# A diffusion-transformer block: the starting addresses of matmul operands, shifted by unused columns in three pools

## The chip, the cores and the metric

The kernel runs on one core of one Trainium2 chip. The metric is the device time of one execution in microseconds (us). A core has TensorE (PE, with its weight loads shown apart as PEld), VectorE (DVE), ScalarE (ACT), GpSimd (POOL) and SyncE (SP, which here issues nearly all DMAs). SBUF is the core's working memory of 128 partitions; a tile takes the same bytes at the same address in every partition. An address below is the offset in bytes within a partition.

## The reference, cut to what matters

One layer, 2048 latent tokens of 1024 channels, preceded by 256 context tokens that only feed the state of the scan:

```
proj = (x * (1 + scale1) + shift1) @ w_in              # input projection
mix  = concat([conformer_conv(proj), ssd_both_directions(proj), pool_mixer(proj)])
x    = layer_norm(ALPHA * x + gate1 * (mix @ w_out))   # output projection
h    = x * (1 + scale2) + shift2
val, gate = split(h @ w_up)                            # up projection, 2 x 2816 columns
f    = (val * gelu(depthwise_conv_3x3(gate))) @ w_down # down projection
out  = layer_norm(ALPHA * x + gate2 * f)
```

Everything is in float32.

## The kernel before

Tokens go in four chunks of 512. A first sweep (`sweep1`, `chunk`, up to about 740 us) makes the input projection chunk by chunk, runs the convolutions on VectorE, the forward scan and the pooling, and parks results in DRAM. A second sweep runs backwards over the chunks: the backward scan (`bwd`), then the output projection and the first layer norm (`mix`). From about 1080 us the feed-forward part (`ffn_chunk`) follows, chunks 3, 2, 1, 0: for each of 22 blocks `f` of 128 columns the gate (`ug`) and the value (`uv`) of the up projection, with the depthwise convolution on VectorE (`fa`) between them; then for each half of the output columns the down projection (`d`) over the 22 blocks into four PSUM banks, then the second layer norm.

Each float32 product is made of three matmuls. `split` cuts an operand into a high part in the type that TensorE takes in one pass (`F32R`) and a remainder (ScalarE copies, GpSimd subtracts; for `gl` VectorE subtracts), and `mm3` multiplies high by high (L108), high by low (L109) and low by high (L110). Names say which: `wh`/`wl` are the halves of a weight tile, `hhi`/`hlo` of the activations of the input projection, `yah`/`yal` and `ybh`/`ybl` of the mixers' outputs, `h2h`/`h2l` of the activations of the up projection, `gh`/`gl` of the gated product. `proj` and the up projection hold the weights stationary (128 columns at a time) and move 512 columns of activations. `mix` and the down projection hold the activations stationary and move 512 columns of weights.

The instructions of every engine are ordered by the scheduler of the framework when the kernel is built. Tiles come from pools; a pool gives each tag its slots one behind the other, and pools stack from the low end or, with `side="right"`, from the high end. All weights go through `load_w` and the pool `wp`, whose slots start at 64 modulo 256. A slice of an operand starts a multiple of 256 bytes into its tile (512 k for a block of 128 columns, 2048 for half of a weight tile, 256 for the row of tokens ahead of a chunk), so an operand's place modulo 256 is that of its tile. In the built programs the operands of the four projections stand at:

| matmuls | stationary | moving | modulo 256 before | modulo 256 after |
|---|---|---|---|---|
| input projection `ps_x`, `ps_z`, `ps_a`, `ps_g`, `ps_p`, `ps_cx` | `wh`, `wl` | `hhi`, `hlo` (pool `p1`) | 64 and 0 | 64 and 64 |
| output projection `o` | `yah`, `yal`, `ybh`, `ybl` (pools `p2`, `pa`) | `wh`, `wl` | 160 and 64 | 64 and 64 |
| up projection `ug`, `uv` | `wh`, `wl` | `h2h`, `h2l` (pool `p3`) | 64 and 64 | 64 and 64 |
| down projection `d` | `gh`, `gl` (pool `p4`) | `wh`, `wl` | 224 and 64 | 64 and 64 |

The other tiles of these pools move along: in `p1` by 64 bytes up (`gl`, `pb`, `zt` and the mixers' weights), in `p2` and `pa` by 96 down (`xt`, `yfr`, `ngr` and others), in `p4` by 160 down (`g`, `r` and the rows of the layer norm). The matmuls of the small projection `dt_c` have 40 stationary columns whose slices are 160 bytes apart. The tiles of the activations are 2048 bytes apart in `p1`, `p2`, `pa` and `p4`; those of the up projection hold 576 columns and are 2304 bytes apart.

Of the kernel before, what the change touches and what calls it, by code (L numbers as in the profile page):

```python
# [7 lines left out]
F32 = mybir.dt.float32  # L8
# [5 lines left out]
P = 128  # L14
# [34 lines left out]
class Kern:  # L49
# [3 lines left out]
    def run(self):  # L53
        tc, t = self.tc, self.t
        with ExitStack() as es:
            self.cp = es.enter_context(tc.tile_pool(name="cp", bufs=1))
            self.wp = es.enter_context(tc.tile_pool(name="wp", bufs=2))
            self.lp = es.enter_context(tc.tile_pool(name="lp", bufs=2))
            self.mm = es.enter_context(tc.tile_pool(name="mm", bufs=4, space=PSUM))
            for n, b in (("si", 1), ("so", 2), ("lo", 1)):  # L60
                setattr(self, n, es.enter_context(tc.tile_pool(name=n, bufs=b, space=PSUM)))
            self.consts()
            e1, e2, e3 = ExitStack(), ExitStack(), ExitStack()
            self.sp = e1.enter_context(tc.tile_pool(name="sp", bufs=2))
            self.ssd_consts()
            e4, e5 = ExitStack(), ExitStack()
            self.pc = e5.enter_context(tc.tile_pool(name="pc", bufs=2, side="right"))
            self.mod_first()
            self.p1 = e4.enter_context(tc.tile_pool(name="p1", bufs=2))
            self.sweep1()  # L70
            e5.close()
            self.pa = e2.enter_context(tc.tile_pool(name="pa", bufs=2, side="right", reuse_waits="tile"))
            self.ngr = self.row(self.pa, t["norm_row"], "ngr")
            top = self.bwd(NCH - 1)
            e4.close()
            self.p2 = e2.enter_context(tc.tile_pool(name="p2", bufs=2, side="right", reuse_waits="tile"))
            last = self.sweep2(top)
            e1.close()
            self.p3 = e3.enter_context(tc.tile_pool(name="p3", bufs=2, reuse_waits="tile"))
            self.mix(*last)  # L80
            pre = self.ffn_pre()
            e2.close()
            self.p4 = e3.enter_context(tc.tile_pool(name="p4", bufs=2, side="right", reuse_waits="tile"))
            self.ffn(pre)
            e3.close()

    def bank(self, pool, name):
        return pool.tile([P, 512], F32, tag="b", name=name)

    def col(self, n, i):  # L90
        return self.cols[:, COFF[n] + i : COFF[n] + i + 1]
# [960 lines left out]
```

## Time and profile before

| | us |
|---|---|
| median of 3 runs (lowest to highest) | 2638.94 (2635.89 to 2642.15) |
| the profiled execution, its own time | 2638.48 |
| span in its trace, first to last instruction | 2636.8 |
| TensorE busy | 2430.4 (92% of the span) |
| VectorE busy | 1849.2 (70%) |
| GpSimd busy | 1330.7 (50%) |
| ScalarE busy | 1145.9 (43%) |
| mean granted clock of TensorE | 0.96 of full speed |

The times are of the whole execution; the trace is of one execution, and its span lacks what lies before the first and behind the last instruction. Busy time of TensorE runs from the start of a matmul to its end, and matmuls overlap: one of 512 columns lasts 0.39 us in the trace and the next starts before it ends. What a matmul costs in a stream is therefore read from the distance between two starts, not from its length. A granted clock of 1.00 is 2.4 GHz, one of 0.50 is 1.2 GHz.

### The profile page before, as it was taken

What the parts mean: (1) busy time and instruction counts of PE and PEld (TensorE: products, weight loads), DVE (VectorE), ACT (ScalarE), POOL (GpSimd) and SP (SyncE); (2) the same over time, 40 slices, a digit from 0 to 9 for tenths busy, and PEclk for the clock granted to TensorE, in tenths of its full rate; (3) what the DMA queues carried; (4) which work ended last, traced back from release to release, by engine and by line L of the source; (5) the groups of instructions that cost most, each with busy time, mean ns of one, the idle gap of its engine ahead of it and who ended that gap; (6) DMA issues with size and microseconds to landing.
All of it is one profiled execution on the core that took longest, in us unless ns stands there. A gap on an engine that the chain in (4) does not pass through costs nothing.

```text
span 2636.8 us, 31624 instructions
## 1 busy us (share of the span) xinstructions
PE 2430.4 (92%) x11338; PEld 1983.4 (75%) x11338; DVE 1849.2 (70%) x2681; ACT 1145.9 (43%) x1761; POOL 1330.7 (50%) x928
## 2 busy tenths in 40 slices
PE   6897999899767988899999999999999999899996
PEld 3776767677656766789998878888878888788885
DVE  5898978689966686576555496665696654876645
ACT  2656565756454333433334333344333343233332
POOL 2555464554524555554446455464454464555444
PEclk7998999999978999899999999999999999999998
DMA  7645343333336565562224343343333343433332
GB/s 281 209 151 170 101 133 124 120 119 111 116 124 211 180 212 189 175 212 92 88 88 131 91 149 97 98 125 100 120 127 97 97 120 94 146 96 104 96 98 70
DMA packets 125838, 347.01 MB, mean 132 GB/s; under 512 B 19680, under 2 KB 24176, under 8 KB 125680
## 3 DMA queue, kind: packets, MB, share of 16 engines
q1 hardware_dynamic: 121072, 336.60, 40.0%
q10 hardware_dynamic: 4608, 8.39, 1.1%
q8 instruction: 89, 1.46, 0.2%
q14 instruction: 69, 0.57, 0.1%
HBM read 298.63 MB, written 46.31 MB: 131 GB/s over the span
## 4 chain that ended last, share of the span: by engine, by line
PE 58%; DVE 23%; ACT 5%; DMA 5%; issue 4%; POOL 3%; SPq 0%; ACTq 0%; POOLq 0%; DVEq 0%
PE d L109 6%; PE d L108 6%; PE d L110 6%; PE uv L108 5%; PE uv L110 5%; PE uv L109 5%; PE ug L108 5%; PE ug L110 5%; PE ug L109 5%; DVE ca_f L256 2%; DVE ca_b L256 2%; DVE c31p L582 2%; DVE fa L876 1%; ACT E_f L345 1%; DVE xt L773 1%
## 5 line engine op out<-in xcount | busy, mean ns | idle before, releaser
L876 DVE SCALAR_TENSOR_TENSOR fa<-gbuf,cols,fa 128x512 f32<-128x512 f32 x704 | 523.5, 753 | 223.9 <-ACT fa L872 201.4
L906 DVE TENSOR_TENSOR gl<-g,gh 128x512 fp32r<-128x512 f32 x176 | 196.2, 1124 | 231.1 <-ACT gh L905 213.9
L96 POOL TENSOR_TENSOR wl_d<-wr_d,wh_d 128x1024 fp32r<-128x1024 f32 x88 | 218.1, 2479 | 227.0 <-ACT wh_d L95 227.0
L96 POOL TENSOR_TENSOR wl_uv<-wr_uv,wh_uv 128x1024 fp32r<-128x1024 f32 x88 | 221.8, 2521 | 203.7 <-ACT wh_uv L95 203.7
L108 PE MATMUL ug<-h2h,wh_ug 128*128 128x512 f32 (+3 forms) x880 | 308.5, 351 | 14.5 <-DVE g L884 10.6
L96 POOL TENSOR_TENSOR wl_ug<-wr_ug,wh_ug 128x1024 fp32r<-128x1024 f32 x88 | 215.1, 2444 | 189.1 <-ACT wh_ug L95 189.0
L109 PE MATMUL ug<-h2l,wh_ug 128*128 128x512 f32 (+3 forms) x880 | 307.4, 349 | 0.0
L110 PE MATMUL ug<-h2h,wl_ug 128*128 128x512 f32 (+3 forms) x880 | 307.1, 349 | 0.0
L108 PE MATMUL uv<-h2h,wh_uv 128*128 128x512 f32 x704 | 275.7, 392 | 10.0 <-DVE g L884 10.0
L109 PE MATMUL d<-wl_d,gh 128*128 128x512 f32 x704 | 280.6, 399 | 0.0
L108 PE MATMUL d<-wh_d,gh 128*128 128x512 f32 x704 | 277.3, 394 | 0.0
L109 PE MATMUL uv<-h2l,wh_uv 128*128 128x512 f32 x704 | 275.4, 391 | 0.0
L110 PE MATMUL uv<-h2h,wl_uv 128*128 128x512 f32 x704 | 275.2, 391 | 0.0
L110 PE MATMUL d<-wh_d,gl 128*128 128x512 f32 x704 | 266.0, 392 | 0.0
L905 ACT ACTIVATE gh<-g 128x512 fp32r<-128x512 f32 x176 | 110.9, 630 | 261.5 <-PE d L109 240.1
L108 PEld LDWEIGHTS ug<-h2h,wh_ug 128*128 128x128 f32 x880 | 167.4, 190 | 34.7 <-DVE g L884 11.8
L95 ACT ACTIVATE wh_ug<-wr_ug 128x1024 fp32r<-128x1024 f32 x88 | 93.2, 1059 | 220.1 <-PE uv L109 193.3
L109 PEld LDWEIGHTS ug<-h2l,wh_ug 128*128 128x128 f32 x880 | 167.3, 190 | 17.8
L110 PEld LDWEIGHTS ug<-h2h,wl_ug 128*128 128x128 f32 x880 | 167.2, 190 | 16.8
L582 DVE SCALAR_TENSOR_TENSOR c31p<-gl,cols,c31p 128x512 f32<-128x512 f32 x232 | 161.8, 745 | 12.2 <-ACT c31p L579 12.0
L108 PEld LDWEIGHTS uv<-h2h,wh_uv 128*128 128x128 f32 x704 | 132.8, 189 | 37.8 <-DVE g L884 11.0
L108 PEld LDWEIGHTS d<-wh_d,gh 128*128 128x128 f32 x704 | 132.1, 188 | 34.3
(388 smaller groups left out, 5536.7 us busy)
## 6 DMA issues: line engine op xcount, KB each, us to landing
wr_ug<-in_w_up SPq DMA_DIRECT2D x88, 512.0 KB, 3.6
wr_uv<-in_w_up SPq DMA_DIRECT2D x88, 512.0 KB, 3.6
wr_d<-in_w_dn SPq DMA_DIRECT2D x88, 512.0 KB, 3.5
wm<-in_w_mod SPq DMA_DIRECT2D x64, 256.0 KB, 3.6
wr_x<-in_w_x SPq DMA_DIRECT2D x32, 512.0 KB, 3.7
wr_o<-in_w_o SPq DMA_DIRECT2D x32, 512.0 KB, 4.2
wm<-in_w_mod SPq DMA_DIRECT2D x16, 512.0 KB, 8.3
x_c<-in_xT SPq DMA_DIRECT2D x32, 256.0 KB, 3.4
```

The lines of the kernel that those rows point to most:

```text
L95: nc.scalar.activation(hi, src, AF.Copy)
L96: nc.gpsimd.tensor_tensor(lo, src, hi.bitcast(F32), AL.subtract)
L108: nc.tensor.matmul(out, a[0], b[0], start=first, stop=False)
L109: nc.tensor.matmul(out, a[0], b[1], start=False, stop=False)
L110: nc.tensor.matmul(out, a[1], b[0], start=False, stop=last)
L256: nc.vector.scalar_tensor_tensor(acc[:, :n], raw[:, off : off + n], wk, acc[:, :n], AL.mult, AL.add)
L345: nc.scalar.activation(E[:, h, :], E[:, h, :], AF.Relu, bias=cum[:, d, s, h : h + 1], scale=-1.0)
L582: nc.vector.scalar_tensor_tensor(to[:, :m], gl[:, j, o + k : o + k + m], w[k], acc[:, :m], AL.mult, AL.add)
L773: nc.vector.scalar_tensor_tensor(xs[i][:, hsl], xs[i][:, hsl], ALPHA, m, AL.mult, AL.add)
L876: nc.vector.scalar_tensor_tensor(acc, G[:, dr : dr + 8, dc : dc + GW], wc[i], acc, AL.mult, AL.add)
L905: nc.scalar.activation(gh, gt[k], AF.Copy)
L906: nc.vector.tensor_tensor(gl, gt[k], gh.bitcast(F32), AL.subtract)
```

## The change

Three tiles that nothing writes or reads are added, each with a name of its own and one slot: 64 bytes in `p1`, 96 bytes in `pa`, 160 bytes in `p4`. The `p1` tile is the first of its pool, so that all others start 64 bytes later. `pa`, `p2` and `p4` grow from the high end, and the tile added there moves the tiles of the pool, and of the pool that stacks on it, 96 or 160 bytes down.

```diff
             self.p1 = e4.enter_context(tc.tile_pool(name="p1", bufs=2))
+            self.shift(self.p1, 64)
             self.sweep1()
...
             top = self.bwd(NCH - 1)
+            self.shift(self.pa, 96)
             e4.close()
...
             self.ffn(pre)
+            self.shift(self.p4, 160)
             e3.close()
...
+    def shift(self, pool, n):
+        pool.tile([P, n // 4], F32, name="shift", bufs=1)
```

In the built programs every engine has the same instructions in the same order with the same waits before and after (10767 on TensorE, 2683 on VectorE, 1779 on ScalarE, 933 on GpSimd, 849 on SyncE); the source lines behind the added ones shift by 2 to 6, and the addresses differ as the table above says. No row of the order stands here, since none differs in more than its line.

## Rows read from the trace of the kernel before

**Rows 1.** The page: its span, and busy us (share of the span) of TensorE.
```profile
span 2636.8 us, 31624 instructions
...
PE 2430.4 (92%) x11338; PEld 1983.4 (75%) x11338; DVE 1849.2 (70%) x2681; ACT 1145.9 (43%) x1761; POOL 1330.7 (50%) x928
```

**Rows 2.** The chain of waits over the whole span: shares by engine and line.
```profile
by line: PE d L109 6.2%; PE d L108 6.1%; PE d L110 6.1%; PE uv L108 5.2%; PE uv L110 5.1%; PE uv L109 5.1%; PE ug L108 5.0%; PE ug L110 5.0%; PE ug L109 5.0%; issue 4.1%; DVE ca_f L256 2.5%; DVE ca_b L256 2.4%; DVE c31p L582 2.0%; DVE fa L8
```

**Rows 3.** TensorE's timeline, up projection: start us, us, operation; 132 matmuls apart.
```profile
1660.05 0.39 PE L110 MATMUL ug<-h2h,wl_ug 128*128 128x512 f32 x1
...
1689.97 0.39 PE L110 MATMUL uv<-h2h,wl_uv 128*128 128x512 f32 x1
```

**Rows 4.** TensorE's timeline, down projection: 120 matmuls apart.
```profile
1771.53 0.39 PE L108 MATMUL d<-wh_d,gh 128*128 128x512 f32 x1
...
1799.53 0.39 PE L108 MATMUL d<-wh_d,gh 128*128 128x512 f32 x1
```

**Rows 5.** TensorE's timeline, input projection: 24 matmuls apart.
```profile
451.95 0.39 PE L110 MATMUL ps_x<-hhi_c,wl_x 128*128 128x512 f32 x1
...
457.55 0.39 PE L110 MATMUL ps_x<-hhi_c,wl_x 128*128 128x512 f32 x1
```

**Rows 6.** TensorE's timeline, output projection: 18 matmuls apart.
```profile
884.43 0.40 PE L108 MATMUL o<-wh_o,yah 128*128 128x512 f32 x1
...
888.65 0.40 PE L108 MATMUL o<-wh_o,yah 128*128 128x512 f32 x1
```

**Rows 7.** The same at half clock, 3 matmuls apart, and the window's PEclk.
```profile
861.50 0.63 PE L110 MATMUL o<-wh_o,yal 128*128 128x512 f32 x1
...
862.78 0.63 PE L110 MATMUL o<-wh_o,yal 128*128 128x512 f32 x1
...
core 0: us, PE busy (x) PEld busy (x) DVE busy (x) ACT busy (x) POOL busy (x), PEclk, DMA share, GB/s
860.50:863.00 2.50, 2.50 (x7) 1.92 (x7) 2.50 (x4) 1.01 (x1) 1.81 (x2) 0.50 0.95 336
```

**Rows 8.** Groups by form: `d` on L109 (busy us, mean ns); L108, L110 count alike.
```profile
L109 PE MATMUL d<-wl_d,gh 128*128 128x512 f32 x704 | 280.6, 399 | 0.0
```

**Rows 9.** TensorE's timeline, 448 columns in the last chunk: 21 matmuls apart.
```profile
2399.89 0.36 PE L110 MATMUL ug<-h2h,wl_ug 128*128 128x448 f32 x1
...
2404.15 0.36 PE L110 MATMUL ug<-h2h,wl_ug 128*128 128x448 f32 x1
```

**Rows 10.** Windows, a stretch of `d` alone: length, then columns as in rows 7.
```profile
1770.00:1860.00 90.00, 90.00 (x388) 72.39 (x387) 43.79 (x45) 37.35 (x51) 46.49 (x21) 1.00 0.38 112
```

**Rows 11.** Waits from 1760 to 1900: waiter, releaser, total us, times, longest.
```profile
ACT gh L905 <- PE d L109: 56.8, 33, 4.7
```

**Rows 12.** The chain in order of time behind the last `d` of chunk 3.
```profile
1508.45 0.24 PE d L110
1508.72 0.69 DVE fm L920
```

**Rows 13.** The chain's shares in windows 112:740, 228:300, 380:430 and 740:1076, in this order.
```profile
by line: DVE ca_f L256 10.3%; DVE ca_b L256 10.0%; DVE c31p L582 8.4%; issue 8.4%; ACT E_f L345 4.0%; DVE c31t L582 2.7%; PE ps_z L110 2.3%; PE ps_z L109 2.2%; PE ps_z L108 2.2%; POOL hlo_c L96 2.2%; DMA E_f<-scr_arow 1.7%; ACT L346 1.6%; D
by line: DMA x_c<-in_xT 9.1%; POOL hlo_c L96 8.3%; PE ps_x L108 6.2%; PE ps_x L110 6.1%; issue 5.9%; PE ps_x L109 5.8%; PE ps_a L110 5.2%; PE ps_a L108 5.2%; PE ps_a L109 5.2%; PE yd_f L408 4.7%; ACT E_f L345 3.2%; PE pl L665 2.8%; PE ps_g 
by line: DMA E_f<-scr_arow 10.9%; issue 9.4%; POOL hlo_c L96 9.2%; PE ps_a L108 8.2%; PE ps_a L109 7.1%; PE ps_a L110 6.9%; POOL wl_g L96 4.7%; ACT E_f L345 4.2%; PE ps_g L108 3.7%; PE ps_g L110 3.7%; PE ps_g L109 3.7%; ACT x_c L234 3.5%; P
by line: issue 8.0%; DVE xt L773 5.3%; DMA yac<-scr_yac 4.4%; DVE st_l L790 3.8%; PE o L108 3.8%; PE o L109 3.4%; DVE E_b L359 3.2%; DMA yfr<-scr_yf 3.0%; PE o L110 2.9%; PE st_b L390 2.7%; DVE mix L772 2.7%; DMA E_b<-scr_arow 2.6%; DMA xt<
```

**Rows 14.** TensorE's timeline, 256 columns: context 15 apart, up projection 21 apart.
```profile
79.15 0.28 PE L110 MATMUL ps_cx<-hhi_ctx,wl_cx 128*128 128x256 f32 x1
...
80.85 0.28 PE L110 MATMUL ps_cx<-hhi_ctx,wl_cx 128*128 128x256 f32 x1
...
1201.40 0.28 PE L110 MATMUL ug<-h2h,wl_ug 128*128 128x256 f32 x1
...
1203.92 0.28 PE L110 MATMUL ug<-h2h,wl_ug 128*128 128x256 f32 x1
```

## The prediction

> **What bounds the kernel now.** I read the page's busy times first: TensorE is busy 2430 of 2637 us [rows 1], so the question is whether the change makes its matmuls shorter, and where TensorE sets the end. The chain of waits answers the second: the down projection alone, `d`, holds 6.2 + 6.1 + 6.1 = 18.4% of the span, 485 us, and the up projection (`ug`, `uv`) some 30% more [rows 2]. Then I read TensorE's timeline for the one thing that the change could touch, the distance from the start of one matmul to the start of the next in an unbroken stream.
>
> All the streams in question are the same instruction: 128 rows, 128 stationary columns, 512 moving columns. The up projection starts one every (1689.97 - 1660.05) / 132 = 226.7 ns [rows 3]. The down projection starts one every (1799.53 - 1771.53) / 120 = 233.3 ns [rows 4], the input projection every (457.55 - 451.95) / 24 = 233.3 ns [rows 5], the output projection every (888.65 - 884.43) / 18 = 234.4 ns [rows 6]. Where the granted clock is 0.50, after a wait, the output projection takes (862.78 - 861.50) / 3 = 426.7 ns [rows 7], which is 512 columns at 1.2 GHz with nothing over. At 2.4 GHz the columns alone would be 213.3 ns, so at the full clock each matmul has 13.3 ns over in the up projection and 20.0 to 21.1 ns in the three others. The overhead does not scale with the clock, so it is not the array's own work; it looks like operands that arrive too slowly.
>
> Now the placement in the section on the kernel: in the up projection both operands start at 64 modulo 256; in the three others one starts at 64 and the other at 0, 160 or 224. The input projection and the up projection are the same code (`mm3` with the weights stationary, the same weight slots, the same PSUM pool), and they differ only in where the activations lie. So the trace of before already holds the experiment that the change makes on the other three.
>
> **The change part by part.** No instruction is added, removed or reordered, and every wait is as before; the only thing that changes is the address of the tiles of `p1`, `p2`, `pa` and `p4`. So nothing new can queue, and the sum is a length per matmul times the matmuls on the path.
>
> - Down projection. 704 matmuls on each of three lines, 2112 in all [rows 8]. If they go from 233.3 to 226.7 ns, all of them give 2112 x 6.67 ns = 14.1 us. On the chain they hold 485 us, so 485 x 20/700 = 13.9 us reaches the end. I take 13.9. The lower bound comes from a place where equal addresses gained less: the 448-column matmuls of the up projection in the last chunk run at (2404.15 - 2399.89) / 21 = 202.9 ns, 16.2 over their 186.7 [rows 9]; with 16.2 over, `d` would gain 3.8 ns each, 8.0 us.
>  Does the gain stay? In a stretch of 90 us that is nothing but `d`, TensorE is busy all 90 while VectorE is busy 43.8, ScalarE 37.4 and GpSimd 46.5 [rows 10], and it is ScalarE that waits for `d` to free the buffers of `gh`, 56.8 us in 140 [rows 11]. The feeders have room for a stream that is 3% faster. Behind the last `d` of a chunk the chain goes on through `fm` on VectorE [rows 12], which starts that much earlier.
> - Input projection. 18 tiles x 4 chunks x 8 x 3 = 1728 matmuls of 512 columns, at most 1728 x 6.67 = 11.5 us. But in the sweep the chain is VectorE's convolutions above all [rows 13]. What these rows show of it on the chain is `ps_z` 6.7% of 628 us, 42 us; `ps_x` and `ps_a` 33.7% of 72 us, 24 us; `ps_a` and `ps_g` 33.3% of 50 us, 17 us. Of these 83 us, 20/700 is 2.4 us. I take that; the bounds are 0 (the other engines take over) and 11.5.
> - Output projection. 768 matmuls, at most 768 x 7.7 = 5.9 us; on the chain 10.1% of 336 us, 34 us [rows 13], of which 7.7/234.4 is 1.1 us. I take 1.1; the bounds are 0 and 5.9.
> - Context tiles. Here the rule runs the other way. At 256 columns the input projection with 0 against 64 starts one every (80.85 - 79.15) / 15 = 113.3 ns, and the up projection with equal addresses one every (1203.92 - 1201.40) / 21 = 120.0 ns [rows 14]. If the 144 context matmuls go to 120, that is 1.0 us, partly on the path; I take half, 0.5 us lost.
> - The rest. The transposes `yt` (64) and `ht` (128) now have both operands at 160 and get 64 against 160; even at 6.7 ns each that is 1.3 us, taken at nothing, because their stage waits for others [rows 13]. The 96 matmuls of `dt_c` have slices at eight different places before and after: nothing. VectorE, ScalarE and GpSimd read and write the same tiles at a new place; in `d` they have the room of [rows 10], and I have no row that shows them depend on it: nothing.
>
> Sum: 13.9 + 2.4 + 1.1 - 0.5 = 16.9 us. The profiled execution took 2638.5 us (the median of the three runs is 2638.9, so it stands for them). 2638.5 - 16.9 = 2621.6, 0.64% less. A measurement of this kernel tells about 0.2%, 5.3 us, from no change.
>
> A rule speaks against all of this. The overhead over 213.3 ns in [rows 3 to 6], and its absence at the half clock in [rows 7], say that two streams of operands do get in each other's way. The Trainium skill (page "SBUF — State Buffer", section "Who interferes with whom") gives TensorE two independent read ports, one for the moving operand and one for the weight load, and says that TensorE never waits on anyone; "TensorE: Matmul & The Clock Gate", section "Back-to-back issue gap", gives columns over clock plus 2.5 ns, an estimate of 215.8 ns for 512 columns wherever they lie. By these pages the sum would be nothing, and the time 2638.5. The trace disagrees on the gap (226.7 and 233.3), so the ports are less free than that here.
>
> **The rivals.**
> 1. No change: place modulo 256 isn't the cause. The activations of the up projection are also 2304 bytes apart (576 columns), those of the three others 2048; a cause in the higher bits of the address would fit [rows 3 to 6] as well, and the change leaves those bits nearly alone. Against it: within the up projection the higher bits differ from one k to the next, and the interval does not. Time 2638.5, with the rest of the list within 2 us of it.
> 2. Slower: equal places collide. [rows 14] show it at 256 columns: +6.7 ns where the addresses are equal. If at 512 columns with the roles swapped (in `d` the activations are stationary and the weights stream) the overhead goes up a step instead of down, 2112 x 6.67 = 14.1 us are lost in `d` and 1.1 in the output projection, with 2.4 gained in the input projection as in the sum: 2638.5 + 12.8 + 0.5 = 2651.8. It decides if `d` starts one matmul less often than every 233.3 ns. Against it: 30 us of [rows 3] at 512 columns without an exception.
> 3. All of it comes through: the projections' gain isn't lost beside VectorE, because the chain there changes hands often. 14.1 + 11.5 + 5.9 - 0.5 = 31.0 us, 2607.5. Against it: only 17 us of the chain's 50 us by [rows 13] is TensorE's projections where `ps_a` and `ps_g` are at their densest.
> 4. Part of it: the streams fall into the pattern of [rows 9]. The three matmul terms shrink to 3.8/6.67: 17.4 x 0.57 - 0.5 = 9.4 us, 2629.1.
>
> **How the numbers follow.** The forecast (interval falls to about 226.7 in `d`, 13 to 24 us gained) 0.70; rival 4 0.10; rival 3 0.04; rival 1 0.11; rival 2 0.05. Forecast, 3 and 4 are faster by over 0.2%: 0.84; rival 1 is within 0.2%: 0.11; rival 2 slower: 0.05. The forecast's own range is 2614 to 2627. The range that should hold 8 in 10 goes down to rival 3, 2608, and up past rival 4 to 2636; outside lie rivals 1 and 2.
>
> **What would show each step.** In the timeline of the changed kernel, `d` should start a matmul every 226.7 ns (680 for a triple instead of 700), and the same for `ps_x`, `ps_z` and `o` where they run unbroken at the full clock; at the half clock they should stay at 426.7. Context matmuls at 120 ns. Mean length of the three `d` groups lower by some 6 ns each, and the up projection's as before. A 90 us stretch of `d` should still show TensorE busy throughout; if idle time appears in it, the feeders were the cover I misjudged. From the start of the first `ug` to the end the stretch should be 14 us shorter, and from the start to there about 3 us. I would be wrong if `d` stays at 233.3 (rival 1), rises (rival 2), or if the interval falls and the end doesn't move.

## The result and the profile after

| us | before | changed |
|---|---|---|
| median of 7 runs each | 2642.15 | 2629.33 |
| lowest to highest | 2635.89 to 2646.07 | 2621.35 to 2632.03 |
| the profiled execution, its own time | 2638.48 | 2625.29 |
| span in its trace | 2636.8 | 2623.6 |

The ratio of the two kernels is 0.9948 with a 95% interval of 0.9932 to 0.9964. Of 2642 us that is 13.7 us less, 9.5 to 18.0. The forecast was 16.9 us less, 2621.6 us. The time lies inside the range of 2608 to 2636 and 2 us above the 2614 to 2627 that the forecast's own mechanism was given. The kernel before stood at 2642.15 here, 3.7 us above the 2638.5 from which the sum was made.

The page of the changed kernel answers to [rows 1]; the second line is the head of the chain of waits over the whole span, which answers to [rows 2]. The source lines of `mm3` are now L114 to L116 (before L108 to L110).

```profile
PE 2419.6 (92%) x11338; PEld 1996.2 (76%) x11338; DVE 1840.7 (70%) x2681; ACT 1145.5 (44%) x1761; POOL 1336.3 (51%) x928
...
by line: PE d L114 5.8%; PE d L116 5.8%; PE d L115 5.8%; PE ug L114 5.3%; PE ug L115 5.3%; PE ug L116 5.3%; PE uv L114 5.2%; PE uv L115 5.2%; PE uv L116 5.1%; issue 4.1%; DVE ca_f L262 2.3%; DVE ca_b L262 2.3%; DVE fa L882 1.4%; DVE c31p L5
```

The same instructions were executed. The down projection holds 17.4% of the chain instead of 18.4%, and its place as the longest item did not pass to another engine.

TensorE's timeline of the changed kernel (start us, us, operation) shows what became of the streams of [rows 4], [rows 5], [rows 6] and the context part of [rows 14]. The pairs of rows are 131, 36, 15 and 15 matmuls apart.

```profile
1770.03 0.39 PE L114 MATMUL d<-wh_d,gh 128*128 128x512 f32 x1
...
1799.72 0.39 PE L114 MATMUL d<-wh_d,gh 128*128 128x512 f32 x1
```
```profile
449.50 0.39 PE L116 MATMUL ps_x<-hhi_c,wl_x 128*128 128x512 f32 x1
...
457.66 0.39 PE L116 MATMUL ps_x<-hhi_c,wl_x 128*128 128x512 f32 x1
```
```profile
887.12 0.40 PE L114 MATMUL o<-wh_o,yah 128*128 128x512 f32 x1
...
890.53 0.39 PE L114 MATMUL o<-wh_o,yah 128*128 128x512 f32 x1
```
```profile
79.25 0.28 PE L116 MATMUL ps_cx<-hhi_ctx,wl_cx 128*128 128x256 f32 x1
...
81.04 0.28 PE L116 MATMUL ps_cx<-hhi_ctx,wl_cx 128*128 128x256 f32 x1
```

Dividing the distance by the count gives 226.6 ns in `d` (before 233.3), 226.7 in the input projection (233.3), 227.3 in the output projection (234.4) and 119.3 at 256 columns (113.3). From here on a stream is given by its triple, the time from one product of `mm3` to the next three matmuls later, as the mean over all unbroken triples at the full clock: `d` went from 700.0 to 680.2 ns in every chunk, the input projection from 699.9 to 683.8, `o` from about 702 to 685, context from 346.3 to 359.0. The up projection stayed at 680 in the two inner chunks.

At half clock nothing changed. In the same timeline the output projection, just behind a wait, starts three matmuls in (862.69 - 861.41) / 3 = 426.7 ns, as in [rows 7].

```profile
861.41 0.63 PE L116 MATMUL o<-wh_o,yal 128*128 128x512 f32 x1
...
862.69 0.63 PE L116 MATMUL o<-wh_o,yal 128*128 128x512 f32 x1
```

The group of `d` by form answers to [rows 8]: a mean of 389 ns instead of 399.

```profile
L115 PE MATMUL d<-wl_d,gh 128*128 128x512 f32 x704 | 273.9, 389 | 0.0
```

And the stretch of `d` that [rows 10] show: windows of the changed kernel, length, then busy us (count) of PE, PEld, DVE, ACT and POOL, the clock, DMA share and GB/s. With it the two sweeps.

```profile
112.00:740.00 628.00, 559.64 (x2556) 443.83 (x2557) 542.44 (x841) 366.95 (x599) 335.87 (x243) 0.93 0.42 132
740.00:1076.00 336.00, 276.68 (x1347) 225.04 (x1346) 231.04 (x425) 141.62 (x287) 165.31 (x124) 0.88 0.54 176
1770.00:1860.00 90.00, 90.00 (x398) 74.47 (x397) 44.29 (x46) 37.62 (x52) 47.61 (x20) 1.00 0.37 111
```

TensorE is still busy all of the 90 us, with 398 matmuls in place of 388. So the feeders keep up with the faster stream there.

Where did the time come from? In the traces the four stretches of `d`, first start to last end, took 123.36 us each before, 493.4 in all; now 120.58, 119.87, 120.41 and 119.86, 480.7 in all, 12.7 us less. From the first `ug` to the end it is 1520.22 against 1507.61, 12.6 us less. From the start to the first `ug` it is 1116.55 against 1115.96, only 0.6 us less, where the forecast had 3. The two traces aren't alike there in the clock: up to the first `ug` TensorE had the half clock for 167 us before and for 201 us in the changed kernel.

### The profile page after: what moved, and what is told of

The parts are those of the page before. It is cut to its first block, busy times and chain, and to the rows that moved or that the text cites. A ratio compares the mean times of both kernels' runs of the same rounds, so it can differ in the third digit from the quotient of the medians.

```text
span 2623.6 us, 31624 instructions
## 1 busy us (share of the span) xinstructions
PE 2419.6 (92%) x11338; PEld 1996.2 (76%) x11338; DVE 1840.7 (70%) x2681; ACT 1145.5 (44%) x1761; POOL 1336.3 (51%) x928
## 4 chain that ended last, share of the span: by engine, by line
PE 59%; DVE 21%; DMA 6%; ACT 6%; issue 4%; POOL 3%; SPq 0%; ACTq 0%; POOLq 0%; DVEq 0%
PE d L114 6%; PE d L116 6%; PE d L115 6%; PE ug L114 5%; PE ug L115 5%; PE ug L116 5%; PE uv L114 5%; PE uv L115 5%; PE uv L116 5%; DVE ca_f L262 2%; DVE ca_b L262 2%; DVE fa L882 1%; DVE c31p L588 1%; ACT E_f L351 1%; DMA wm<-in_w_mod 1%
## 5 line engine op out<-in xcount | busy, mean ns | idle before, releaser
L114 PE MATMUL ug<-h2h,wh_ug 128*128 128x512 f32 (+3 forms) x880 | 309.3, 351 | 17.2 <-DVE g L890 10.6
L115 PE MATMUL ug<-h2l,wh_ug 128*128 128x512 f32 (+3 forms) x880 | 308.7, 351 | 0.0
L116 PE MATMUL ug<-h2h,wl_ug 128*128 128x512 f32 (+3 forms) x880 | 308.2, 350 | 0.0
L114 PE MATMUL uv<-h2h,wh_uv 128*128 128x512 f32 x704 | 275.6, 391 | 8.8 <-DVE g L890 8.5
L115 PE MATMUL uv<-h2l,wh_uv 128*128 128x512 f32 x704 | 275.3, 391 | 0.0
L116 PE MATMUL uv<-h2h,wl_uv 128*128 128x512 f32 x704 | 274.9, 390 | 0.0
L114 PE MATMUL d<-wh_d,gh 128*128 128x512 f32 x704 | 274.0, 389 | 0.6 <-ACT fg L884 0.4
L115 PE MATMUL d<-wl_d,gh 128*128 128x512 f32 x704 | 273.9, 389 | 0.0
L116 PE MATMUL d<-wh_d,gl 128*128 128x512 f32 x704 | 263.7, 389 | 0.0
L114 PEld LDWEIGHTS ug<-h2h,wh_ug 128*128 128x128 f32 x880 | 168.3, 191 | 37.6 <-DVE g L890 11.9
L115 PEld LDWEIGHTS ug<-h2l,wh_ug 128*128 128x128 f32 x880 | 168.2, 191 | 17.8
L116 PEld LDWEIGHTS ug<-h2h,wl_ug 128*128 128x128 f32 x880 | 168.4, 191 | 16.7
L114 PEld LDWEIGHTS uv<-h2h,wh_uv 128*128 128x128 f32 x704 | 132.9, 189 | 36.7 <-DVE g L890 9.2
L101 ACT ACTIVATE wh_uv<-wr_uv 128x1024 fp32r<-128x1024 f32 x88 | 93.2, 1059 | 145.5 <-PE ug L115 89.8
```

The lines of the kernel that those rows point to most:

```text
L101: nc.scalar.activation(hi, src, AF.Copy)
L114: nc.tensor.matmul(out, a[0], b[0], start=first, stop=False)
L115: nc.tensor.matmul(out, a[0], b[1], start=False, stop=False)
L116: nc.tensor.matmul(out, a[1], b[0], start=False, stop=last)
```

## The experiments

The theory: a stream of these three-matmul products runs at 680 ns where both operands start at the same place modulo 256, and slower elsewhere; what `d` gains reaches the end, what the sweeps gain mostly doesn't. Diffs are against the changed kernel. "Before" is the kernel before on the same chip in the same session.

### Each part alone

```diff
 # p4 alone (p1 alone and pa alone likewise: the two other lines are left out)
-            self.shift(self.p1, 64)
-            self.shift(self.pa, 96)
```

> The 160 bytes in p4 alone; p1 and p2/pa lie as before. Theory (the down projection carries the whole gain): a triple of d takes 680 ns as in the changed kernel, those of ps and o 700 and 702 as before, and the time is 12 to 13 us under before (ratio about 0.9952), the same as with all three. Rival (the two sweeps give a part of the gain, 3 to 4 us of it, and the run is only noisy): 0.9963 or more, clearly behind the changed kernel.

> The 64 bytes in p1 alone. Theory: triples of ps at 512 columns fall from 700 to some 684 ns, the context's at 256 columns rise from 346 to 359, d and o stay; the time is that of before within 0.1% (ratio 0.999 to 1.001), since the first sweep ends with VectorE and transfers and not with the projections. Rival (prediction's sum): 1.9 us gained, 0.9993; rival 3 of the prediction: 10.5 us, 0.996.

> The 96 bytes in pa alone, which move p2 too. Theory: triples of o fall from 702 to some 685 ns, all others stay; time of before within 0.1%. Rival (the prediction's sum): 1.1 us gained, 0.9996; rival (something else in p2 or pa gets slower with its new place and eats the gain of the first sweep): 1.001 or more.

| kernel | median us (runs) | ratio to before, interval | `d` triple | input triple | `o` triple |
|---|---|---|---|---|---|
| before | 2641.30 (23) | | 700.0 | 699.9 | 702 |
| `p4` alone | 2627.85 (6) | 0.9951, 0.9937 to 0.9965 | 680.2 | 699.8 | 702 |
| `p1` alone | 2642.75 (12) | 0.9997, 0.9985 to 1.0009 | 700 | 683.4 | 702 |
| `pa` alone | 2641.24 (12) | 1.0004, 0.9992 to 1.0017 | 700 | 699.9 | 685 |

Each shift shortens its own stream at 512 columns and no other (`p1` alone also lengthens the context tiles, as in the whole change). `p4` alone gives 12.9 us, as much as the whole change within the intervals, and in its trace the four stretches of `d` are 479.5 us long, 13.9 us shorter than before. The two others aren't told apart from nothing: `p1` alone lies between 4.0 us gained and 2.4 lost, `pa` alone between 2.1 gained and 4.5 lost. The 1.9 and 1.1 us that the forecast gave them (2.4 less 0.5 for context, and 1.1) lie inside these intervals, so they are neither shown nor excluded.

One reason why so little can be seen there is the clock. Windows of the kernel before, of the one with `p4` alone and of the one with `pa` alone, over the first sweep, in which neither shift changes anything (columns as in the windows above):

```profile
112.00:740.00 628.00, 559.86 (x2557) 436.34 (x2558) 544.12 (x842) 368.54 (x604) 332.04 (x243) 0.95 0.42 132
```
```profile
112.00:740.00 628.00, 565.86 (x2564) 441.68 (x2564) 544.14 (x845) 370.01 (x609) 334.51 (x243) 0.94 0.42 132
```
```profile
112.00:740.00 628.00, 566.34 (x2557) 441.30 (x2556) 545.09 (x844) 369.76 (x607) 331.88 (x243) 0.94 0.41 132
```

The granted clock there is 0.95 before, 0.94 in the two others and 0.93 in the changed kernel. Summed over the window, TensorE had the half clock for 57 us before, 70 and 78 in these two, 85 in the changed kernel.

The mean granted clock of each run was measured too, and the time goes with it. Among the 23 runs of the kernel before, the six at 0.957 or more have a median of 2639.8 us and the five at 0.952 or less one of 2645.4; the correlation over all 23 is -0.77. The mean over the runs was 0.9548 before, 0.9543 with `p4` alone, 0.9539 with `p1` and 0.9535 with `pa`. A straight line through these 53 runs, with one slope for all four kernels (13 us per 0.01 of clock), gives an estimate of the gains at equal clock: 13.9 us for `p4` alone (give or take 2.1), 1.3 for `p1` (1.7) and 1.7 for `pa` (1.7). So the two small gains may be there, hidden by a slightly lower clock. Whether the shifts themselves lower the clock isn't tested.

### What about the place counts

In one kernel each half of `d` in each chunk got another place for `gh` and `gl`, and each chunk another for `hhi` and `hlo`; weights stay at 64. In the first, places go in steps of 32 bytes:

```diff
+        off = {"c0": 8, "c1": 16, "c2": 24, "c3": 32}.get(name, 0)
-            hi = p1.tile([P, 512], F32R, tag="hhi", name=f"hhi_{name}_{k}", bufs=8)
+            hi = p1.tile([P, 576], F32R, tag="hhi", name=f"hhi_{name}_{k}", bufs=8)[:, off : off + 512]
...
+            off = 8 * (2 * (NCH - 1 - c) + hf)
-                    gh = p4.tile([P, 512], F32R, tag="gh", name=f"gh{c}_{hf}_{k}", bufs=3)
+                    gh = p4.tile([P, 576], F32R, tag="gh", name=f"gh{c}_{hf}_{k}", bufs=3)[:, off : off + 512]
```

(`hlo` and `gl` likewise.)

> The changed kernel with the tiles of gh and gl 64 columns wider and used from another column in each chunk and half, so that the stationary operand of d lies at 64, 96, 128, 160, 192, 224, 0, 32 modulo 256 in the order of the run, against moving weights at 64; and the tiles of hhi and hlo likewise, so that the moving operand of the input projection lies at 96, 128, 160, 192 in chunks 0 to 3. Theory (the two places must be equal modulo 256): only the first half of chunk 3 has triples of 680 ns in d, the seven other halves 700; ps at 700 in all chunks. Rival (what counts is whole 64-byte blocks, or an even number of them): 680 also at 128, 192 and 0, or at 192 alone. Rival (the overhead goes with the distance, with a still better place somewhere): other values than 680 and 700, some under 680. Time about 10 us over the changed kernel under the theory.

The second takes finer steps, with the same edit and other numbers:

```diff
+        off = {"c0": 4, "c1": 12, "c2": 40, "c3": 60}.get(name, 0)
...
+            off = (1, 2, 4, 6, 12, 48, 52, 60)[2 * (NCH - 1 - c) + hf]
```

> As the scan before, with finer and other steps: the stationary operand of d at 68, 72, 80, 88, 112, 0, 16, 48 modulo 256 in the order of the run against moving weights at 64, and the moving operand of the input projection at 80, 112, 224, 48 in chunks 0 to 3. Theory (the difference moving minus stationary modulo 256 sets the overhead, in both roles alike; 0 gives 680 ns for a triple, +64 gives 687): the half at 0 repeats 687 (686 to 688); the input projection's chunks at +16 and the half at 48 (also +16) agree with each other within 3 ns, as do the chunk at +48 and the half at 16 (also +48). Rival (roles or places count by themselves): the pairs differ. Is equality sharp? If the memory is read in pieces of 16 bytes or more, 68 and 72 still give 680; if the start itself must be equal, 700.

Windows of 50 us of the first kernel, `d` alone, at places 64, 96, 128, 160, 192, 224, 0 and 32 in this order (columns: length, PE, PEld and DVE busy with their counts, clock, DMA share, GB/s):

```profile
1400.00:1450.00 50.00, 50.00 (x223) 41.39 (x222) 0.00 (x0) 1.00 0.43 133
1460.00:1510.00 50.00, 50.00 (x216) 40.28 (x215) 0.00 (x0) 1.00 0.30 95
1770.00:1820.00 50.00, 50.00 (x216) 40.35 (x215) 0.00 (x0) 1.00 0.40 124
1832.00:1882.00 50.00, 50.00 (x216) 40.21 (x215) 0.00 (x0) 1.00 0.30 94
2140.00:2190.00 50.00, 50.00 (x217) 40.55 (x216) 0.00 (x0) 1.00 0.36 113
2202.00:2252.00 50.00, 50.00 (x216) 40.23 (x215) 0.00 (x0) 1.00 0.31 95
2503.00:2553.00 50.00, 50.00 (x220) 41.07 (x219) 0.00 (x0) 1.00 0.31 95
2564.00:2614.00 50.00, 50.00 (x216) 40.21 (x215) 0.00 (x0) 1.00 0.24 74
```

TensorE is busy all of every window, so the count of matmuls that touch it is the rate: 222 or 223 in 50 us is 226 ns each, 216 is 233. Only the first window, where both operands start at 64, has the fast rate; the seventh, at place 0, comes next with 220. Two windows of the second kernel, at places 72 and 80:

```profile
1460.00:1510.00 50.00, 50.00 (x219) 40.71 (x218) 0.00 (x0) 1.00 0.32 95
...
1770.00:1820.00 50.00, 50.00 (x222) 41.38 (x222) 0.00 (x0) 1.00 0.45 134
```

The triples of both kernels, by place:

| place of `gh`, `gl` (weights moving at 64) | triple ns | place of `hhi`, `hlo` (weights stationary at 64) | triple ns |
|---|---|---|---|
| 64 | 680.0 | 64 (changed kernel) | 683.8 |
| 68 | 697.2 | 48 | 707.7 |
| 72 | 692.0 | 80 | 695.2 |
| 80 | 680.1 | 96 | 699.9 |
| 88 | 690.0 | 112 | 698.0 |
| 96, 128, 224 | 699.9 to 700.1 | 128 | 688.1 |
| 112 | 699.9 | 160 | 700.0 |
| 160 | 702.8 | 192 | 697.9 |
| 192 | 697.4 | 224 | 702.2 |
| 0 (in both kernels) | 686.7 | 0 (before) | 699.9 |
| 16, 32, 48 | 695.5, 700.1, 685.0 | | |

In steps of 64 bytes it is the difference, moving less stationary, that counts, in either role: +64 gives 686.7 and 688.1, +128 gives 697.4 and 697.9, -64 gives 700.1 and 699.9. In finer steps that rule, the theory of the second scan, fails: +16 gives 685.0 in `d` (place 48) and 695.2 in the input projection (place 80), and -16 gives 680.1 in `d` (place 80), as fast as equal places, and 707.7 in the input projection (place 48), the slowest of all. The theory of the first scan, 680 at equality and 700 elsewhere, was too simple as well. Four bytes off (68) lose most of the gain, sixteen bytes off in one direction (80) lose none. So equality is enough for 680 but isn't the only place that has it, and no place was faster. Against the kernel before, the two scans took 2642.96 (2641.30) and 2638.30 (2644.96) once each; by their `d` triples, whose means are 695.9 and 690.8, (700 - 695.9) x 704 = 2.9 us and 6.5 us less were due.

Then the same with everything at another place, 96 for all operands:

```diff
+            self.shift(self.wp, 32)
-            self.shift(self.pa, 96)
+            self.shift(self.pa, 64)
-            self.shift(self.p4, 160)
+            self.shift(self.p4, 128)
```

> All operands of the four projections at 96 modulo 256 instead of 64 (32 unused bytes ahead of the weights' slots, 64 instead of 96 and 128 instead of 160 in the other pools). Theory (equality counts, not the place 64): triples of 680 ns in d, uv and ug as in the changed kernel, and its time. Rival (whole 64-byte blocks count, which 96 is not): 700 in all of them, and a time some 30 us longer.

It took 2629.81 us in one run, against 2644.96 before. Triples are as in the changed kernel: `d` 680.0 to 681.4, up projection 680, input 683.5, `o` 685. A window of `d` (columns as in the scans):

```profile
1770.00:1820.00 50.00, 50.00 (x222) 41.36 (x222) 1.64 (x3) 1.00 0.43 126
```

So equal places give the fast rate at 96 as at 64; 64 as such isn't needed.

Last, only the low half of the gated product moved, to 160, with the high half at 64:

```diff
-                    gl = p4.tile([P, 512], F32R, tag="gl", name=f"gl{c}_{hf}_{k}", bufs=3)
+                    gl = p4.tile([P, 576], F32R, tag="gl", name=f"gl{c}_{hf}_{k}", bufs=3)[:, 24:536]
```

> The changed kernel with gl alone at 160 modulo 256 and gh at 64, so that in each triple of d two stationary operands are equal in place with the moving weights and one is not. Theory (a matmul is slowed by the weight load that runs beside it, the next one's): the interval of the matmul ahead of the one with gl (high by low, L115) takes most of the rise, and the triple lies between 680 and 700, near 687. Rival (a matmul's own stationary operand counts): the interval of the third matmul (L116) rises. Rival (one unequal load sets the stream's whole rhythm): 700.

One run took 2639.89 us, against 2645.34 before. The triple of `d` is 697.1 to 697.5: one load in three at an unequal place takes back 17 of the 20 ns. A window of `d`, with that of the changed kernel, which has 222 matmuls in it, in the second fence:

```profile
1770.00:1820.00 50.00, 50.00 (x217) 40.45 (x216) 0.00 (x0) 1.00 0.41 125
```
```profile
1770.00:1820.00 50.00, 50.00 (x222) 41.36 (x221) 2.63 (x4) 1.00 0.39 118
```

The distance behind each of the three lines grew, L114 from 226.6 to 232.5, L115 from 226.8 to 231.2, L116 from 226.8 to 232.6, though the loads of two of them are where they were. So the three don't pay each for itself, and the triple is far from the 687 of the theory; the rival by which one unequal load sets the whole rhythm (700) comes nearest. Which load meets which stream isn't settled.

### The up projection made unequal

```diff
     # ahead of the other tiles of p3
+            self.shift(self.p3, 96)
```

> The changed kernel with 96 unused bytes at the head of p3, which take the equality away from the up projection (moving at 160 against 64), the only projection that had it before. Theory: its 512-column triples go from 680 to 700 ns, 1056 of them, 21.1 us; the 256-column triples of chunk 3 go the other way, as the context did in the first comparison, from 360 to 341 or so (176 of them, 3.3 us); the 320 and 448 columns are not known. Time 15 to 24 us over the changed kernel, slower than before by 2 to 11 us. Rival (the gain came from something else that moved in p4): the up projection stays at 680 and the time at that of the changed kernel.

2645.45 us (10 runs) against 2644.96: ratio 1.0005, 0.9994 to 1.0017. That is 0.57 points above the changed kernel's ratio, some 15 us (0.0057 x 2643): making the up projection unequal takes back the whole gain. TensorE's timeline in the up projection (`uv` and `ug` take turns in it), 132 matmuls apart:

```profile
1660.70 0.40 PE L117 MATMUL uv<-h2h,wl_uv 128*128 128x512 f32 x1
...
1691.50 0.40 PE L117 MATMUL uv<-h2h,wl_uv 128*128 128x512 f32 x1
```

(1691.50 - 1660.70) / 132 = 233.3 ns, where [rows 3] had 226.7 on the same code and the same 2304 bytes from tile to tile. The narrow matmuls were the miss: the triple at 448 columns went from 608.5 to 615.9 only, at 320 from 439.4 to 440.1, and at 256 from 359.5 to 359.8, where a fall to 341 was expected after the context tiles of [rows 14]. The places of the two cases differ, too: moving less stationary is -64 in those context tiles and +96 here, so what 256 columns do at -64 in the up projection isn't tested. Work added on TensorE: 176 triples per chunk and projection, x 20 ns for four of them, x 16 for two, x 7 for the one at 448 columns, 21 us. In the trace 16.5 us of it come out between the first `ug` and the end: the up projection passes on most, but not all, of what its stream loses.

### How much of the sweep's work reaches the end

First more work: the input projection of the changed kernel put at the worst place found, 48.

```diff
-            hi = p1.tile([P, 512], F32R, tag="hhi", name=f"hhi_{name}_{k}", bufs=8)
+            hi = p1.tile([P, 576], F32R, tag="hhi", name=f"hhi_{name}_{k}", bufs=8)[:, 60:572]
```

(`hlo` likewise.)

> The changed kernel with the moving operand of the input projection at 48 modulo 256 instead of 64 (tiles of hhi and hlo 64 columns wider, used from column 60), all instructions in the same order. The fine scan showed triples of 708 ns there, against 684 in the changed kernel: 24 ns on 576 triples, 14 us of TensorE's work added, with no change of order. Theory (the leaving-out run was so fast partly because the scheduler had ordered the work otherwise; the projections' length hardly reaches the end): at most 3 us over the changed kernel, ratio to before up to 0.996. Rival (half of the projections' length reaches the end, as 22 of 46 us did in the leaving-out run): 6 to 7 us over the changed kernel, ratio about 0.9975.

TensorE's timeline of the input projection in this kernel, 36 matmuls apart, 236.7 ns each:

```profile
449.11 0.40 PE L114 MATMUL ps_x<-hhi_c,wh_x 128*128 128x512 f32 x1
...
457.63 0.40 PE L114 MATMUL ps_x<-hhi_c,wh_x 128*128 128x512 f32 x1
```

2630.59 us (6 runs) against 2645.34: ratio 0.9945, 0.9930 to 0.9959. The triple of the input projection is 704.8 instead of 683.8 ns in the mean, which on 576 triples is 12 us more of TensorE's work, and the time is that of the changed kernel: 0.9945 against 0.9948, 0.8 us less, give or take 5.7. The 6 to 7 us of the rival would have given 0.9975, outside the interval; a cost of 2 or 3 us would not be seen.

Then less work: for the latent tokens, columns 320 to 511 of the product low by high are left out (so part of the projection is missing), with the three products in another order, since one of them is now shorter:

```diff
-            self.mm3(ps[:, :n], a, [v[:, :n] for v in hs[k]], k == 0, k == KD - 1)
+            nc, h, m = self.nc, hs[k], 320 if n == 512 else n
+            nc.tensor.matmul(ps[:, :n], a[0], h[0][:, :n], start=(k == 0), stop=False)
+            nc.tensor.matmul(ps[:, :m], a[1], h[0][:, :m], start=False, stop=False)
+            nc.tensor.matmul(ps[:, :n], a[0], h[1][:, :n], start=False, stop=(k == KD - 1))
```

> The changed kernel with 192 of 512 columns left out of one of the three matmuls of each triple in the input projection of the latent tokens (the product of the weights' remainder with the activations' high part, columns 320 to 511): four times the change's saving there, 80 ns on each of 576 triples, 46 us of TensorE's work. The scheduler orders some instructions otherwise for it, which by itself may move the time by some us. Theory (the first sweep doesn't end with TensorE): under 5 us of the 46 reach the end against the changed kernel. Rival (the chain's share of TensorE there, 83 us of 403 us of these matmuls, passes on to the end as the prediction summed it): 9 to 10 us.

2607.52 us (4 runs): ratio 0.9859, 0.9837 to 0.9881, some 23 us under the changed kernel's ratio (0.0089 x 2643, give or take 7). That is more than either side expected, and TensorE saved less than the 46 us that were expected: the triple fell from 683.8 to 619 ns, which on 576 triples is 37 us. In the one trace, of the slowest of the four executions (2615.46 us), the first `ug` starts at 1106.91 instead of 1115.96, 9.1 us earlier. As the scheduler moved thousands of instructions for the shorter product, I ran the same order with all 512 columns:

```diff
-            self.mm3(ps[:, :n], a, [v[:, :n] for v in hs[k]], k == 0, k == KD - 1)
+            nc, h = self.nc, hs[k]
+            nc.tensor.matmul(ps[:, :n], a[0], h[0][:, :n], start=(k == 0), stop=False)
+            nc.tensor.matmul(ps[:, :n], a[1], h[0][:, :n], start=False, stop=False)
+            nc.tensor.matmul(ps[:, :n], a[0], h[1][:, :n], start=False, stop=(k == KD - 1))
```

> The control of the leaving-out run: the changed kernel with the three products of the input projection in the order in which that run had them (low by high before high by low), all with their 512 columns, nothing left out. The scheduler orders the work anew for it. Theory (order made a good part of that run's 22 us): 5 us or more under the changed kernel. Rival (order makes nothing): that of the changed kernel within 3 us.

2626.85 us (4 runs): ratio 0.9940, 0.9919 to 0.9962, not told apart from the changed kernel. So the order of the products alone doesn't explain it, but the scheduler's order isn't the same in these two either. Left open: whether 37 us less passes on more than half while 12 us more passes on little or nothing, or whether the schedule that came with the shorter product is better by itself.

No kernel of these computes the whole layer faster than the changed one; `p4` alone, all at 96, the input projection at 48 and the other order are level with it.

## Why the prediction was right, and where it was off

**The interval: right.** `d` starts a matmul every 226.6 ns, the input projection every 226.7, `o` 227.3, and context moved the other way, to 119.3 where 120 was said. The up projection of the kernel before was the right model for the others. Why unequal places are slow isn't shown: the prediction took it that operands arrive too slowly, and the runs show that the interval depends on the two places, no more. Rival 1, that place isn't the cause but the 2304 bytes from tile to tile, falls with the up projection made unequal: 233.3 at the same 2304. Rival 2, that equal places collide where the activations are stationary, falls with `d` itself. Rival 4 gave almost the time that came out, 2629.1, but by another way: its 3.8 ns per matmul appeared nowhere in `d`, which gained 6.7, and the nearness is luck: the kernel before stood 3.7 us higher here, and the 3 us of the sweeps didn't show.

**The term of the down projection: right.** 13.9 us were said, from 20/700 of the chain's 485 us. The trace of the changed kernel shows 12.7 us less in `d`, that of `p4` alone 13.9, and the time of `p4` alone 12.9, with an interval of 9.2 to 16.6. The cover of [rows 10] held: 90 of 90 us busy.

**The terms of the sweeps: not settled.** This is the step that may be mis-sized. Input projection 2.4, output projection 1.1 and context -0.5 made 3.0 us of the sum; the trace shows 0.6 up to the first `ug`, and the whole change, 13.7, is as much as `p4` alone. None of these excludes 3.0 by itself, and the estimate at equal clock, 1.3 and 1.7, comes to as much as the forecast.

The kernel with the input projection at 48 doesn't decide it. A share of 20/700 on 83 us of chain is a rate of 2.4 in 11.5, a fifth, and by it 12 us more work would have cost 2.5; it measured -0.8, give or take 5.7, which leaves room for 2.5 as for nothing. So the rate lies between nothing and four tenths there, and all of it coming through (rival 3) is excluded. The kernel with columns left out passed on more, 23 of 37 us, but in another order of instructions.

Two parts of the working were loose. The lines of [rows 13] end before the list does, so the 83 us aren't all: in the whole chain of the kernel before, the input projection holds 98 us between 112 and 740 us, 2.8 us by the same share. And none of the context's matmuls stands in that chain, so the 0.5 us for them had no row behind it. The chain's share of an engine says where the end was set in that one execution; how much of a change passes on, it doesn't measure.

**The lower bound.** The 8.0 us for `d`, from the 448 columns of [rows 9], was no guide to 512: in the up projection made unequal, the narrow matmuls hardly react to the one other place tried, 160 (7 ns in a triple at 448 columns, under 1 at 320 and 256).

A rule was weighed against the forecast. The Trainium skill (page "SBUF — State Buffer", section "Who interferes with whom") gives TensorE two independent read ports and no wait on anyone; it says nothing of places, and read as the prediction read it, the place of an operand could change nothing. The runs here disagree with that reading, 226.7 against 233.3 ns for the same instruction by address alone, and the measurement decides. The 215.8 ns that the prediction took beside it from the Trainium skill (page "TensorE: Matmul & The Clock Gate", section "Back-to-back issue gap") stand there as the gap of an isolated matmul, not of a stream with a weight load for each, so they were no rule for these streams.

## What to carry to other kernels

If two streams of the same matmul start at different intervals, compare where their operands lie modulo 256 bytes before looking for a wait; here one line of unused columns gave 3% on such a stream, and only where TensorE alone sets the end, in the down and the up projection, was it seen in the time. Put all operands of a product at the same place, the low half too, because one of three that lies elsewhere takes back nearly all of it. And where several engines share a stage, a gain of a few us is about as large as what the clock moves from run to run: compare runs at equal clock, and test the stage by a run that makes it longer or shorter without changing the order, before trusting the engine's share of the chain.

## What the runs showed of the hardware that was not expected

- The place matters in steps far finer than 64 bytes, and not alike for the two operands: with the moving one at 64 a triple takes 697.2 ns with the stationary one at 68 and 680.1 at 80; the same difference as in the latter, -16, with the moving one at 48 and the stationary one at 64, takes 707.7, the slowest mean in the table.
- A difference of +64 is nearly as good as none (686.7 and 688.1), -64 as bad as most (700).
- It goes away at half clock (426.7 ns before and after, in the output projection), and in the up projection at 256 and 320 columns (359.5 against 359.8, 439.4 against 440.1, moving at 64 and 160), while context at 256 columns is slower at equal places (359.0 against 346.3, moving at 64 and 0). Whether the place or something else sets these apart is open.
- TensorE's time at half clock in the two sweeps together was 127 us in the kernel before, 165 in the changed one, 178 with `p1` alone and 140 with the other order of products, in one execution each. Within one kernel, the time of a run goes with its mean granted clock, some 12 us for 0.01 in the 23 runs of the kernel before. What sets the clock of a run apart from the next isn't shown.
